# Attention steps handed out in groups of two or three between dense products, in a one-core decoder block

## The chip, the core and the metric

The kernel runs on one core of a Trainium2 chip. TensorE (PE in the rows, with PEld for its weight loads) multiplies matrices into PSUM banks; VectorE (DVE), ScalarE (ACT) and GpSimd (POOL) read those banks or SBUF and do the element-wise work; SyncE (SP) issues most transfers. Each engine has its own instruction order and waits on semaphores for the others. The metric is the device time of one execution in microseconds, lower is better: the median of 3 runs before the change is 640.49 us (640.24 to 640.78).

## The reference

One decoder block on 512 tokens of width 1024, all in float32:

```python
hn = rms_norm(x, norm_g)
proj = hn @ w_in                      # q, k, v, forget logits, gate
q = rms_norm(q, q_gain); k = rms_norm(k, k_gain)
o_moba = moba_attention(...)          # heads 0-3
o_fox  = forgetting_attention(...)    # 6 heads
o_dil  = dilated_attention(...)       # 6 heads
y_moba = rms_norm(o_moba); y_fox = rms_norm(o_fox) * sigmoid(g_fox); y_dil = rms_norm(o_dil)
x = x + concat([y_moba, y_fox, y_dil]) @ w_out
x = x + square(relu(rms_norm(x) @ w_up)) @ w_down
```

There are 16 heads of width 64. All three kinds of attention are causal and reduce here to softmax(q k / 8 + a bias per head) v over the 512 tokens, the bias being a table for ten heads and a cumulative sum of log-sigmoids for the six forgetting heads.

## The kernel before, in words

**Dense products.** Every float32 operand is split into a high part and a remainder (whi and wlo for weights, xh and xl, y0h and y0l and so on for activations), and a product is three matmuls: high by high, high by remainder, remainder by high. One k index of one output bank, three matmuls, is called a token here. The generator `product` (L247) yields after each token. Its order is: the first two k for each of four banks in turn, then the middle k, then the last two k for each bank; a bank's `done` function is called after its last token. The input projection is nine chunks of 32 tokens (`IN_CHUNKS`, L41): q and k of four heads (512 columns), v of four heads (256 or 262 columns), in turn, and last the gate g (384 columns). The output projection is four products: 20, 20, 12 and 12 tokens of 512 columns. The first two take k = 0, 1 (group 0 of heads, y0) and k = 5, 6, 7 (group 1, y1); the last two take k = 2, 3, 4 (group 2, y2). Behind it come the up and down products, with no attention between.

**Attention steps.** Each head is 12 steps, each a short run of TensorE work followed by work on other engines:

- stack (two per head, L486): four transposes of q or k, copied by ScalarE;
- s (four, L508): scores of one 128-row block into a bank, bias and minimum on VectorE (L526), exponential on ScalarE (L528), which is the last reader of the bank;
- pt (three, L536): 4, 3 and 3 transposes of the probabilities, copied by ScalarE to pth (L547), remainder by VectorE to ptl (L548);
- av (two, L553): pth and then ptl times v into one bank, copied by ScalarE (L570);
- o (one, L575): four transposes, a sum on VectorE (L582), a product on GpSimd (L589). The o step of a group's last head also calls `group_norm` (L599): squares on ScalarE (L605), a small chain on VectorE (L608, then `rsqrt`), and four row scalings on VectorE (L612 or L616).

Beside these there are y steps, four per group (`y_transpose`, L618: transposes, a ScalarE copy to the high part, L625, a VectorE remainder, L626), and steps with little or no TensorE work (root and norm of q and k, sig, and f for the cumulative sum). A step is written below with head and index, as s 13.2; y 2.3 is the fourth y step of group 2.

**Banks.** All attention steps take their bank from a ring of four ("m"); the dense products take theirs from another four ("acc"). A fifth step can write only when the readers of the first are done.

**The order.** TensorE's order is the program's own; the instructions of the other engines are ordered by the framework's scheduler. After each token the program calls `attend` (L688), a planner that runs when the kernel is built. It keeps a clock of its own (token and step costs), and a step is eligible when the steps that it needs lie a fixed lag back on that clock (`LAG`, L631). A credit grows with each token (1.2 per token of 512 columns in the input projection, in proportion for narrower ones; 2.75 in the output projection) up to 3.0. A TensorE step costs 1.0, a step without TensorE work 0.25. `attend_until` (L700) issues steps with no token between until a named one is out: the o step of the last head of group 1 (head 9) and the y steps of group 1 after the input projection (L761 to L766), and sig and the y steps of group 2 (L770, L771) after the second product of the output projection.

Of the kernel before, what the change touches and what calls it, by code (L numbers as in the profile page):

```python
# [156 lines left out]
def hymba_block(ctx: ExitStack, tc: tile.TileContext, a, out):  # L157
# [513 lines left out]
    credit = 0.0  # L671
    issued = {}

    def eligible(s):
        for key, lag in s[2]:
            if key[1] >= 0:
                if key not in issued or issued[key] + LAG[lag] > clock:
                    return False
        return True

    def issue(s):
        nonlocal clock
        steps.remove(s)
        s[1]()
        clock += COST[s[0][0]]
        issued[s[0]] = clock

    def attend(rate, cost):  # L688

        nonlocal clock, credit  # L690
        clock += cost
        credit = min(credit + rate, 3.0)
        while credit >= 1.0:
            s = next((s for s in steps if eligible(s)), None)
            if s is None:
                return
            issue(s)
            credit -= 1.0 if COST[s[0][0]] else WEIGHT
# [9 lines left out]
    for c, (kind, i) in enumerate(IN_CHUNKS):  # L708
        done = {"g": lambda i: g_done, "qk": lambda i: qk_parts[i][0], "v": v_done}[kind](i)
        n = a[f"w_in{c}"].shape[2]  # L710
        for _ in product(in_first[c], list(range(NK)), in_operands(n), NT, done):
            tokens += 1
            if tokens == STATS_AT:
                x_stats()
            attend(RATE * n / 512, TOKEN * n / 512)
        issued[kind, i] = clock
# [50 lines left out]
    for c, part, ks in OUT_ORDER[:2]:  # L767
        for _ in product(out_first[c, part], ks, out_operands, 4, out_done(c, part)):
            attend(RATE2, TOKEN)
# [250 lines left out]
```

## Time and profile before

| what | us |
| --- | --- |
| median of 3 runs | 640.49 |
| the profiled execution | 639.8 |
| its span, first to last instruction | 638.0 |
| TensorE busy in it | 627.6 |
| VectorE busy in it | 460.2 |
| ScalarE busy in it | 322.4 |

The profiled execution's own time is its span and 1.8 us around it. A timeline row gives the start of the first of a run of like instructions, the time to the end of the last, and in brackets how long the engine was idle before it and who ended that. The ends of matmuls are modelled and overlap the next one's start, so the pace of TensorE is read from start to start.

### The profile page before, as it was taken

What the parts mean: (1) busy time and instruction counts of PE and PEld (TensorE: products, weight loads), DVE (VectorE), ACT (ScalarE), POOL (GpSimd) and SP (SyncE); (2) the same over time, 40 slices, a digit from 0 to 9 for tenths busy, and PEclk for the clock granted to TensorE, in tenths of its full rate; (3) what the DMA queues carried; (4) which work ended last, traced back from release to release, by engine and by line L of the source; (5) the groups of instructions that cost most, each with busy time, mean ns of one, the idle gap of its engine ahead of it and who ended that gap; (6) DMA issues with size and microseconds to landing.
All of it is one profiled execution on the core that took longest, in us unless ns stands there. A gap on an engine that the chain in (4) does not pass through costs nothing.

```text
span 638.0 us, 9834 instructions
## 1 busy us (share of the span) xinstructions
PE 627.6 (98%) x3800; PEld 556.3 (87%) x3800; DVE 460.2 (72%) x786; ACT 322.4 (51%) x575; POOL 43.9 (7%) x63
## 2 busy tenths in 40 slices
PE   7999999999999999999999999999999999999997
PEld 5798898898889998888888989898988989988986
DVE  6794695696688565678899676686578765966872
ACT  7457666676777575549543433343434343433320
POOL 4010210130120100002100000000000000000000
PEclk9999999999999999999999999999999999999999
DMA  8524423323422345167425233422530333212213
GB/s 313 161 96 133 123 84 76 125 75 116 134 63 71 106 136 155 51 230 175 107 72 164 84 111 100 131 68 67 166 100 22 144 100 133 66 37 64 67 43 123
DMA packets 24911, 70.03 MB, mean 110 GB/s; under 512 B 3210, under 2 KB 4762, under 8 KB 24864
## 3 DMA queue, kind: packets, MB, share of 16 engines
q1 hardware_dynamic: 18224, 57.84, 28.5%
q10 hardware_dynamic: 4432, 5.77, 3.7%
q0 software_dynamic: 2208, 5.79, 3.7%
q8 instruction: 30, 0.49, 0.3%
q14 instruction: 17, 0.14, 0.1%
HBM read 61.51 MB, written 2.11 MB: 100 GB/s over the span
## 4 chain that ended last, share of the span: by engine, by line
PE 77%; DVE 7%; ACT 1%; issue 1%; ACTq 0%; POOL 0%; DVEq 0%
PE acc L913 28%; PE m L872 22%; PE acc L274 20%; PE m L514 2%; PE m L565 2%; PE m L541 1%; DVE ptl L548 1%; PE m L495 1%; DVE qkss L400 1%; DVE wlo L119 1%; DVE qks L418 1%; DVE m L526 1%; DVE qkraw L413 1%; DVE qkv L401 1%; DVE osum L582 0%
## 5 line engine op out<-in xcount | busy, mean ns | idle before, releaser
L118 ACT CAST whi<-wraw 128x1024 fp32r<-128x1024 f32 (+3 forms) x66 | 66.7, 1014 | 90.5 <-PE acc L913 39.9
L274 PE MATMUL acc<-whi,xh 128*128 128x512 f32 (+3 forms) x284 | 103.4, 364 | 0.7 <-DVE fl L436 0.4
L913 PE MATMUL acc<-hh,wlo 128*128 128x512 f32 x256 | 101.5, 396 | 0.0
L913 PE MATMUL acc<-hh,whi 128*128 128x512 f32 x256 | 101.3, 396 | 0.0
L913 PE MATMUL acc<-hl,whi 128*128 128x512 f32 x256 | 101.2, 395 | 0.0
L119 DVE TENSOR_TENSOR wlo<-wraw,whi 128x1024 fp32r<-128x1024 f32 (+3 forms) x66 | 78.8, 1195 | 29.6 <-ACT whi L118 28.9
L274 PE MATMUL acc<-wlo,xh 128*128 128x512 f32 (+3 forms) x284 | 95.7, 337 | 2.2 <-DVE wlo L119 2.2
L274 PE MATMUL acc<-whi,xl 128*128 128x512 f32 (+3 forms) x284 | 95.8, 337 | 0.0
L872 PE MATMUL m<-zh,whi 128*128 128x256 f32 x224 | 62.5, 279 | 0.0
L872 PE MATMUL m<-zl,whi 128*128 128x256 f32 x224 | 62.3, 278 | 0.0
L872 PE MATMUL m<-zh,wlo 128*128 128x256 f32 x224 | 62.3, 278 | 0.0
L274 PEld LDWEIGHTS acc<-wlo,xh 128*128 128x128 f32 x284 | 54.0, 190 | 5.3 <-DVE wlo L119 3.0
L274 PEld LDWEIGHTS acc<-whi,xl 128*128 128x128 f32 x284 | 53.6, 189 | 5.1
L913 PEld LDWEIGHTS acc<-hh,wlo 128*128 128x128 f32 x256 | 48.3, 189 | 11.0 <-DVE wlo L119 0.3
L913 PEld LDWEIGHTS acc<-hl,whi 128*128 128x128 f32 x256 | 48.3, 189 | 10.3 <-issue 0.2
L913 PEld LDWEIGHTS acc<-hh,whi 128*128 128x128 f32 x256 | 48.3, 189 | 10.1 <-ACT m L882 0.2
L274 PEld LDWEIGHTS acc<-whi,xh 128*128 128x128 f32 x284 | 53.7, 189 | 3.7 <-DVE vs L430 0.7
L922 DVE TENSOR_TENSOR x<-acc,x 128x512 f32<-128x512 f32 (+1 forms) x65 | 42.6, 676 | 10.3 <-PE acc L913 9.6
L118 ACT CAST whi<-wsum 128x1024 fp32r<-128x1024 f32 x28 | 29.4, 1049 | 40.1 <-PE m L872 40.1
L119 DVE TENSOR_TENSOR wlo<-wsum,whi 128x1024 fp32r<-128x1024 f32 x28 | 34.2, 1221 | 19.6 <-ACT whi L118 19.6
L528 ACT ACTIVATE p<-m,mn 128x128 f32<-128x128 f32 (+1 forms) x64 | 33.6, 527 | 24.6 <-DVE mn L526 22.9
L872 PEld LDWEIGHTS m<-zh,whi 128*128 128x128 f32 x224 | 42.1, 188 | 1.2
(193 smaller groups left out, 1323.5 us busy)
## 6 DMA issues: line engine op xcount, KB each, us to landing
wraw<-in_w_down SPq DMA_DIRECT2D x32, 512.0 KB, 3.6
ublk<-in_w_up SPq DMA_DIRECT2D x28, 512.0 KB, 3.8
wraw<-in_w_in SPq DMA_DIRECT2D x21, 512.0 KB, 3.8
stk<-stk ACTq DMA_DIRECT2D x32, 128.0 KB, 2.4
wraw<-in_w_out SPq DMA_DIRECT2D x6, 512.0 KB, 4.1
alibi<-in_alibi POOLq DMA_DIRECT2D x10, 256.0 KB, 3.0
x<-in_xT SPq DMA_DIRECT2D x4, 512.0 KB, 5.5
wraw<-in_w_up SPq DMA_DIRECT2D x4, 512.0 KB, 5.1
```

Source lines behind the costliest of these rows:

```text
L118: nc.scalar.copy(hi, raw)
L119: nc.vector.tensor_tensor(lo, raw, hi.bitcast(F32), op=ALU.subtract)
L274: nc.tensor.matmul(dst, lhsT=lhs, rhs=rhs, start=(k == 0 and m == 0), stop=(k == n - 1 and m == 2))
L400: nc.vector.tensor_reduce(ss, sq.rearrange("p (h d) -> p h d", d=DH), axis=AX.X, op=ALU.add)
L401: nc.vector.tensor_scalar(state["v"][:, t], ss, 1.0 / DH, eax[:, t : t + 1], op0=ALU.mult, op1=ALU.add)
L413: nc.vector.tensor_tensor(raw, raw, state["y"][:, t].unsqueeze(2).broadcast_to([P, 8, DH]), op=ALU.mult)
L514: nc.tensor.matmul(ps[:, :n], lhsT=st[0][:, i * P : (i + 1) * P], rhs=st[m][:, :n], start=(m == 1), stop=(m == 2 and h < FOX0),)
L528: nc.scalar.activation(p, ps[:, :n], AF.Exp, bias=mn, scale=-1.0, accum_out=st["den"][:, i : i + 1])
L565: nc.tensor.matmul(ot[:, j * P :], lhsT=v, rhs=p, start=(half == 0 and j == 0), stop=(half == 1 and j == 3))
L872: nc.tensor.matmul(acc[:, f * HALF : (f + 1) * HALF], lhsT=lhs, rhs=rhs, start=first and (f, j, m) == (0, 0, 0), stop=(f, j, m) == (1, 3, ...
L913: nc.tensor.matmul(acc, lhsT=lhs, rhs=rhs, start=(p, k, m) == (0, 0, 0), stop=(p, k, m) == (1, 1, 2))
L922: nc.vector.tensor_tensor(dst[:, cols], acc[:, cols], dst[:, cols], op=ALU.add)
```

## The change

`attend` now returns when the credit is below 2.0. A step is handed out only when at least two have come due, and then the loop runs as before, until less than one is left. Rates, costs, lags and the cap are unchanged.

```diff
     def attend(rate, cost):
 
+
         nonlocal clock, credit
         clock += cost
         credit = min(credit + rate, 3.0)
+        if credit < 2.0:
+            return
         while credit >= 1.0:
             s = next((s for s in steps if eligible(s)), None)
```

Three lines are added, so everything below stands three lines further down in the changed kernel (L745 becomes L748).

In TensorE's order, the first attention work is the stacking of heads 0 to 2, in the second q and k chunk (L495 are the transposes of stack steps, four to a step; L274 are tokens of the dense product, three rows to one). Before:

```order
L495 MATMUL m<-identr,qks 128x128 x12
L274 MATMUL acc<-whi,xh 128x512
L274 MATMUL acc<-wlo,xh 128x512
L274 MATMUL acc<-whi,xl 128x512
L495 MATMUL m<-identr,qks 128x128 x4
L274 MATMUL acc<-whi,xh 128x512
L274 MATMUL acc<-wlo,xh 128x512
L274 MATMUL acc<-whi,xl 128x512
L495 MATMUL m<-identr,qks 128x128 x4
```

Now:

```order
L495 MATMUL m<-identr,qks 128x128 x12
L274 MATMUL acc<-whi,xh 128x512
L274 MATMUL acc<-wlo,xh 128x512
L274 MATMUL acc<-whi,xl 128x512
L274 MATMUL acc<-whi,xh 128x512
L274 MATMUL acc<-wlo,xh 128x512
L274 MATMUL acc<-whi,xl 128x512
L495 MATMUL m<-identr,qks 128x128 x8
```

Single steps one token apart have become pairs two tokens apart. Over the whole program the same 205 TensorE steps stand in 94 groups instead of 150, so 111 steps follow another step directly instead of 55.

At TensorE's end of the attention work, in the second product of the output projection (L622 are the transposes of the y steps of group 2, three to a step, y1h and y1l operands of the second product, y2h and y2l of the third), before:

```order
L622 MATMUL m<-ident,o_187 128x128 x9
L274 MATMUL acc<-y1h,whi 128x512
L274 MATMUL acc<-y1l,whi 128x512
L274 MATMUL acc<-y1h,wlo 128x512
L622 MATMUL m<-ident,o_187 128x128 x3
```

Behind these stood three more tokens on y1 and then the first on y2. Now:

```order
L274 MATMUL acc<-y1h,whi 128x512
L274 MATMUL acc<-y1l,whi 128x512
L274 MATMUL acc<-y1h,wlo 128x512
L622 MATMUL m<-ident,o_187 128x128 x12
L274 MATMUL acc<-y2h,whi 128x512
L274 MATMUL acc<-y2l,whi 128x512
L274 MATMUL acc<-y2h,wlo 128x512
```

The four y steps have moved behind the last token on y1 and directly ahead of the first on y2. The o step of head 15, which they need, has moved from 18 tokens ahead of the first y2 token (14, 1 and 3) to 13.

On VectorE at the same place (orr and rs_t belong to the group norm's small chain, L612 scales the rows of o, the x rows add a finished output bank, L626 makes the remainders y2l), now:

```order
L748 TENSOR_TENSOR x_2914<-acc,x_2914 128x512
L289 TENSOR_TENSOR rs_t<-rs_t,orr 128x4
L290 SCALAR_TENSOR_TENSOR orr<-rs_t,orr 128x4
L288 SCALAR_TENSOR_TENSOR rs_t<-orr,ov 128x4
L289 TENSOR_TENSOR rs_t<-rs_t,orr 128x4
L290 SCALAR_TENSOR_TENSOR orr<-rs_t,orr 128x4
L748 TENSOR_TENSOR x_2914<-acc,x_2914 128x512
L612 SCALAR_TENSOR_TENSOR o_187<-o_187,orr,gsig 128x384 x4
L748 TENSOR_TENSOR x_2914<-acc,x_2914 128x512 x2
L626 TENSOR_TENSOR y2l<-m,y2h 128x3x128 x4
```

Before, two weight remainders (L123) stood inside the small chain where two additions to x stand now; the two additions between L612 and L626 stood there before too.

At the other end of the second half, where the input projection ends, the planner has 35 attention steps left to place among the 40 tokens of the first two output products, against 22 before: head 12 from its pt steps on, s 13.3, stack 15.0, s 14.0 to s 14.2 and the first two pt steps of head 13 have slipped past that point. TensorE's order there, now (L622 are the y steps of group 1, L541 the transposes of pt 12.0 to 12.2):

```order
L274 MATMUL acc<-whi,xl 128x384
L622 MATMUL m<-ident,o_186 128x128 x12
L274 MATMUL acc<-y0h,whi 128x512
L274 MATMUL acc<-y0l,whi 128x512
L274 MATMUL acc<-y0h,wlo 128x512
L541 MATMUL m<-ident,p_2842 128x128
L541 MATMUL m<-ident,p_2849 128x128
L541 MATMUL m<-ident,p_2856 128x128
L541 MATMUL m<-ident,p_2873 128x128
```

Before, the o step of head 12 stood directly ahead of these y steps, and the pt step behind the first token was the last one of head 13.

## Rows read from the trace of the kernel before

**Rows 1.** The page: busy time, share of the span and instructions per engine.

```profile
PE 627.6 (98%) x3800; PEld 556.3 (87%) x3800; DVE 460.2 (72%) x786; ACT 322.4 (51%) x575; POOL 43.9 (7%) x63
```

**Rows 2.** Stretches: busy us (instructions) per engine, clock, DMA share, GB/s.

```profile
27.00:236.00 209.00, 207.31 (x1367) 188.08 (x1367) 150.30 (x388) 141.12 (x324) 28.98 (x43) 1.00 0.35 102
236.00:263.30 27.30, 27.25 (x158) 23.16 (x156) 16.96 (x37) 16.96 (x35) 1.83 (x3) 1.00 0.38 117
315.00:638.00 323.00, 319.54 (x1952) 284.77 (x1950) 234.88 (x279) 117.76 (x143) 0.00 (x0) 1.00 0.29 92
```

**Rows 3.** TensorE timeline, two stalls: start, us, instruction, idle before.

```profile
83.80 0.44 PE L514 MATMUL m<-stk,stk 128*128 128x128 f32 x2 [0.39 <-DVE ptl L548]
...
206.82 0.34 PE L274 MATMUL acc<-whi,xl 128*128 128x384 f32 x1
207.75 0.85 PE L565 MATMUL m<-pth,vs 128*128 128x512 f32 x4 [0.59 <-DVE ptl L548]
```

**Rows 4.** TensorE timeline, three stack steps together and one alone.

```profile
48.37 1.15 PE L495 MATMUL m<-identr,qks 128*128 128x128 f32 x12
...
49.65 0.39 PE L274 MATMUL acc<-wlo,xh 128*128 128x512 f32 x1
...
50.11 0.46 PE L495 MATMUL m<-identr,qks 128*128 128x128 f32 x4
...
50.71 0.39 PE L274 MATMUL acc<-wlo,xh 128*128 128x512 f32 x1
```

**Rows 5.** Groups of weight loads on TensorE: busy us, mean ns of one, idle.

```profile
L495 PEld LDWEIGHTS m<-identr,qks 128*128 128x128 f32 x128 | 13.8, 140 | 2.4
```

**Rows 6.** TensorE timeline around the last attention steps.

```profile
262.98 0.60 PE L580 MATMUL m<-ident,ots 128*128 128x128 f32 x4
...
273.04 1.14 PE L622 MATMUL m<-ident,o 128*128 128x128 f32 x9
...
277.12 0.39 PE L274 MATMUL acc<-y2h,whi 128*128 128x512 f32 x1
```

**Rows 7.** The chain that ended last, same stretch: start, us, what.

```profile
263.14 0.44 PE m L580 x4
263.57 9.63 PE acc L274 x42
...
274.88 0.33 PE m L622 x3
```

**Rows 8.** VectorE timeline, same stretch.

```profile
264.23 0.69 DVE L582 TENSOR_REDUCE osum<-m 128x256 f32<-128x512 f32 x1
...
267.81 0.17 DVE L608 TENSOR_SCALAR ov<-oss 128x4 f32<-128x4 f32 x1 [2.90 <-ACT ots L605]
...
271.19 2.21 DVE L612 SCALAR_TENSOR_TENSOR o<-o,orr,gsig 128x384 f32<-128x384 f32 x4
273.32 1.28 DVE L745 TENSOR_TENSOR x<-acc,x 128x512 f32<-128x512 f32 x2
274.52 1.94 DVE L626 TENSOR_TENSOR y2l<-m,y2h 128x384 fp32r<-128x384 f32 x4
```

**Rows 9.** ScalarE timeline, same stretch.

```profile
273.57 1.25 ACT L625 CAST y2h<-m 128x384 fp32r<-128x384 f32 x3 [4.56 <-PE m L622]
275.25 0.48 ACT L625 CAST y2h<-m 128x384 fp32r<-128x384 f32 x1 [0.43 <-PE m L622]
```

**Rows 10.** TensorE timeline where the input projection ends.

```profile
236.06 1.95 PE L622 MATMUL m<-ident,o 128*128 128x128 f32 x12
237.76 0.48 PE L274 MATMUL acc<-y0h,whi 128*128 128x512 f32 x1
...
238.79 0.71 PE L514 MATMUL m<-stk,stk 128*128 128x512 f32 x2
239.34 0.22 PE L519 MATMUL m<-diag,identr 128*128 128x128 f32 x1
239.40 0.44 PE L274 MATMUL acc<-y0h,whi 128*128 128x512 f32 x1
```

**Rows 11.** ScalarE timeline, the exponential of that s step (s 14.3).

```profile
241.13 0.69 ACT L528 ACTIVATE p<-m,mn 128x512 f32<-128x512 f32 x1
```

## The prediction

> **What bounds the kernel now.** I read the busy table first: TensorE is busy for 627.6 of 638.0 us, the next engine, VectorE, for 460.2 [rows 1]. Modelled matmul ends flatter a busy TensorE, so I went on to the stretches. From 27 to 236 us, where attention steps lie between the tokens of the input projection, TensorE is idle for 209.00 - 207.31 = 1.69 us in all; from 236 to 263.3 us it is idle for 0.05 us, and from 315 us on there is no attention left [rows 2]. The granted clock is 1.00 in each. So the attention half is bound by TensorE's own instructions, and VectorE and ScalarE (150 and 141 of 209 us) have room on average. What is left to win there is small. The idle column names four stalls; I take two as samples. One token before s 3.0 can write, the bank that it wants is still read by a pt remainder (idle 0.39), and av 11.0 waits 0.59 for another [rows 3]. A stall costs somewhat more than its idle time: the second has 207.75 - 206.82 = 0.93 from start to start, where a matmul of 384 columns takes 0.18 (0.525 for a token of three), so 0.75 is lost for 0.59 idle [rows 3]. For four stalls that makes 1.69 + 4 x 0.16 = 2.3 us. A fifth loss is not in the idle column: the four y steps of group 1 take 237.76 - 236.06 = 1.70 us where 12 transposes at the 0.11 of other y steps (0.33 for three [rows 7]) take 1.32, so 0.4 us of bank waits [rows 10]. Sum: 2.7 us of waits in the whole attention half.
>
> Third, I looked at what each handover between dense and attention work costs. Three stack steps together: from their start to the second dense matmul 49.65 - 48.37 = 1.28 us, less 0.23 for the dense matmul between, 1.05, or 0.35 a step; one alone: 50.71 - 50.11 - 0.23 = 0.37 [rows 4].
>
> **The change part by part.** No instruction is added or removed; only positions move. SP's and POOL's transfers keep their order but for a bias table some steps earlier or later, and the tables are asked for heads ahead, so I cost them at nothing (cover: the lag of 5.5 planner units between stack and s; if it were gone, one DMA per head would show as an s stall).
>
> (a) *Fewer handovers.* 56 more steps follow another step directly. A joined stack step saves 0.37 - 0.35 = 0.02 us [rows 4]. The other kinds have no shuffle of this size in the rows shown, so I bound them between 0 and 0.02 and take half: 56 x 0.01 = -0.6 us, bounds 0 and -1.1.
>
> The Trainium skill speaks against this term ("TensorE: Matmul & The Clock Gate", section "Step-by-step: what each phase is for"): weight loads are pulled ahead, so that the next weights load while the present matmul runs. A load takes 140 ns [rows 5], and in the run of twelve a transpose takes 1.05 / 12 = 88 ns, so by that rule a step behind another would show some 50 ns that a dense matmul of 512 columns hides: 56 x 0.05 = +2.8 us. The rows have it the other way, -20 ns, so the sum goes by the rows and the rule becomes a rival.
>
> (b) *The end of attention.* This is the largest term. Before: the o step of head 15 starts at 262.98. Its consumers run in a chain: head sum 264.23, squares on ScalarE, the small chain from 267.81, row scalings 271.19 to 273.40, two additions to x to 274.60, the four remainders y2l to 274.52 + 1.94 = 276.46 [rows 8]. So the last y2l is ready 13.5 us after the o step starts. Over this lie 14 + 1 + 3 tokens and four y steps, and the first matmul on y2 starts at 277.12, that is 14.1 us after it [rows 6], and uses y2h; the second uses y2l. There are 0.66 + 0.23 = 0.9 us to spare. Now only 13 tokens lie between, at 9.63 / 42 x 3 = 0.69 us each [rows 7], the o step is 0.44 [rows 7], and four y steps are 4 x 0.33 [rows 7]: TensorE arrives at the first y2 matmul 0.44 + 8.97 + 1.32 = 10.7 us after the o step's start, and at the second at 10.9. The y steps themselves barely wait (the first row scaling is done 271.19 + 0.55 - 262.98 = 8.8 us after the o step, the last 10.4; TensorE reaches them from 9.4 to 10.4). But the chain is as long as before: VectorE has two additions where it had two weight remainders, and the two additions ahead of y2l are still there, the last of them waiting for the last token itself. So y2l is ready at about 13.5, and 13.5 - 10.9 = 2.6 us of TensorE time are lost; nothing dense stands between. Lower bound: if y2l overtook the queue and only y2h counted. Its last copy ended at 275.25 + 0.48 = 275.73 [rows 9], 0.85 us after the last y step's start at 274.88 [rows 7], and where four copies of 0.42 (1.25 / 3) queue behind one another it is some 1.4, so at least 1.2 us with one remainder behind it. Upper bound: 1 us more, if the chain starts behind ScalarE's weight copies: 3.6. I take +2.7.
>
> (c) *The start of the output projection.* 35 steps instead of 22 must go among its tokens, at two or three per single token (rate 2.75), so a step comes back to a bank of the ring of four sooner. A score step frees its bank at the end of its exponential: s 14.3 left TensorE at 239.40 and its exponential ended at 241.13 + 0.69 = 241.82, 2.4 us later [rows 10, 11]. In the new order y 1.3 wants the bank of s 13.2 after one 384-column token and three y steps, 0.52 + 1.0 = 1.5 us; s 14.2 wants that of s 13.3 after stack 15.0, a token and two short s steps, 0.37 + 0.69 + 0.7 = 1.75; pt 13.2 that of s 14.3 after 1.8, s 15.3 that of pt 14.1 after 1.9. Four waits of 0 to 0.9 us; the one of s 14.2 is the worst, since its exponential also stands behind three pt copies. At 2.0 us for a narrower s (0.5), 2.4 (0.65 for s 14.2, 0.6 for pt 13.2) and little for the last (0.1) they make 1.8; the y waits of before, 0.4, are replaced by the first. Net +1.4, bounds 0 (all absorbed, as in the stretch 236 to 263.3 now) and +2.5.
>
> (d) *Inside the input projection.* Of the 2.3 us of stalls, the one before s 3.0 goes (eight tokens now stand between pt 2.2 and it), the others are tied to chunk ends and to VectorE's load and may stay. What is late next: the pattern of three pt steps, two tokens, an s step, an s step, where the second s wants the first pt's bank 2.4 to 2.5 us later; before, 2.55 us was too short once, for s 3.0 [rows 3]. I take -0.3, bounds -2.3 and +3.3 (six such places at 0.55).
>
> Sum: -0.6 + 2.7 + 1.4 - 0.3 = +3.2 us. On the profiled execution's 639.8 (span 638.0 and 1.8 around it) that is 643.0; the median of the runs is 0.7 higher, so I forecast 643.7.
>
> **The rivals.**
>
> *Everything is absorbed and stalls vanish (not slower).* If groups give VectorE and ScalarE longer quiet stretches, all 2.3 us of stalls and the 0.4 at the y steps go, joins save 0.6, (c) is zero, and (b) is at its lower bound: 640.5 - 3.3 + 1.2 = 638.4. For it: VectorE is busy for only 72% of the stretch. Against it: the end of attention is a chain of latencies, not a load. It decides at a y2l ready within 1.2 us of the last y step.
>
> *The tail is at its lower bound and the rest cancels:* 640.5 - 0.6 + 1.2 - 0.3 + 0.2 = 641.0, or less if one more stall goes: within 0.2% of before.
>
> *Groups of three starve the bank ring inside the input projection:* (d) at +3.3 instead of -0.3 makes 647.3. For it is the stall of s 3.0; against it that runs of three pt steps stand in the order of before already and only one of them stalled a successor.
>
> *Exposed weight loads:* +2.8 instead of -0.6 in (a), 140 ns less 88 for every further join [rows 4, 5], makes 647.1; rows 4 speak against it. It is the rule of the skill named above.
>
> That the change does nothing is excluded by the order: 150 groups have become 94.
>
> **How the numbers follow.** Forecast with (b) as worked out and (c) between its bounds: 0.73, own range 642.0 to 645.5. Ring starved: 0.08. Exposed loads: 0.03. Cancelling: 0.10, of which I count two thirds within 0.2% (1.3 us, about what a measurement here can tell from no change) and a third above. All absorbed: 0.06, faster. So slower 0.73 + 0.08 + 0.03 + 0.03 = 0.87, same 0.07, faster 0.06. The range 641.2 to 646.2 leaves out the two long cases, the fast one and a part of the cancelling one, under 0.2 together.
>
> **What would show it.** (b): an idle time of TensorE of 1 to 3 us before the first or second matmul on y2, ended by VectorE's y2l, and none there before. (c): the stretch from the y steps of group 1 to the o step of head 15 longer than its steps and tokens, with idle times ended by L528, L547 or L548. (a): three stack steps still at 1.05 us, two at 0.72. (d): four or fewer stalls of 0.3 to 0.8 us before the y steps of group 1. The prediction is wrong if y2l is ready before TensorE arrives, or if the sum of idle times inside the input projection moves by more than 1.5 us.

## Result and profile after

The changed kernel takes 643.97 us (median of 4 runs, 642.99 to 645.33) against 640.52 for the kernel before: ratio 1.0057, 95% interval 1.0045 to 1.0069. In a second series it took 643.66 (5 runs) against 640.62, ratio 1.0051 (1.0039 to 1.0064). It is slower by 0.5 to 0.6%, about what was forecast (643.7). But of the four terms only two had about the right size; the other two missed in opposite directions. Some executions of the changed kernel took 1.2 to 2.3 us more than others of the same series, no profile fell in one of them, and why they do is open.

The profiled execution took 642.99 us (span 641.2), 3.2 more than that of before. The page's busy times and the stretches that answer to [rows 1, 2] (27 us to the y steps of group 1, and from there to the o step of head 15):

```profile
PE 628.2 (98%) x3800; PEld 556.6 (87%) x3800; DVE 457.8 (71%) x786; ACT 322.9 (50%) x575; POOL 44.1 (7%) x63
```

```profile
27.00:231.30 204.30, 201.98 (x1323) 183.41 (x1323) 143.51 (x374) 134.59 (x305) 28.54 (x42) 1.00 0.35 99
231.30:268.00 36.70, 36.45 (x219) 31.35 (x217) 22.30 (x52) 23.64 (x53) 2.38 (x4) 1.00 0.42 135
```

All engines have the same work as before. In the input projection TensorE is idle for 204.30 - 201.98 = 2.32 us (1.69 before), in the output projection's first stretch for 0.25 (0.05 before), both at granted clock 1.00. What is left lies at the end of attention. TensorE's timeline there (start, us, instruction, idle before and who ended it), which answers to [rows 6]:

```profile
267.60 0.60 PE L580 MATMUL m<-ident,ots 128*128 128x128 f32 x4
...
276.95 1.47 PE L622 MATMUL m<-ident,o 128*128 128x128 f32 x12
279.20 0.51 PE L274 MATMUL acc<-y2h,whi 128*128 128x512 f32 x1 [0.78 <-ACT y2h L625]
280.57 0.50 PE L274 MATMUL acc<-y2l,whi 128*128 128x512 f32 x1 [0.87 <-DVE y2l L626]
```

TensorE comes to the y steps 9.35 us after the o step of head 15 began and then waits twice, for y2h and for y2l. From start to start these two cost 1.03 and 1.15 us more than where nothing waits, 2.17 together. VectorE at the same place, which answers to [rows 8]:

```profile
268.23 0.69 DVE L582 TENSOR_REDUCE osum<-m 128x256 f32<-128x512 f32 x1 [3.63 <-PE m L580]
...
272.11 0.17 DVE L608 TENSOR_SCALAR ov<-oss 128x4 f32<-128x4 f32 x1 [1.23 <-ACT ots L605]
...
275.26 2.20 DVE L612 SCALAR_TENSOR_TENSOR o<-o,orr,gsig 128x384 f32<-128x384 f32 x4
277.38 1.28 DVE L748 TENSOR_TENSOR x<-acc,x 128x512 f32<-128x512 f32 x2
278.57 1.95 DVE L626 TENSOR_TENSOR y2l<-m,y2h 128x384 fp32r<-128x384 f32 x4
```

The chain is that of before, two additions to x ahead of y2l included. It ends at 280.52, 12.9 us after the o step's start (13.5 before), and TensorE's matmul on y2l starts 0.05 us later. ScalarE, which answers to [rows 9], copies y2h behind two weight conversions:

```profile
276.24 1.41 ACT L122 ACTIVATE whi<-wraw,gains 128x512 fp32r<-128x512 f32 x2 [4.16 <-PE acc L274]
277.55 1.60 ACT L625 CAST y2h<-m 128x384 fp32r<-128x384 f32 x4
```

The handovers, TensorE's timeline at two joined stack steps (answers to [rows 4]):

```profile
50.91 0.79 PE L495 MATMUL m<-identr,qks 128*128 128x128 f32 x8
51.54 0.47 PE L274 MATMUL acc<-whi,xh 128*128 128x512 f32 x1
51.85 0.39 PE L274 MATMUL acc<-wlo,xh 128*128 128x512 f32 x1
```

51.85 - 50.91 - 0.23 = 0.71 us for two, where two single ones took 0.74.

Inside the input projection the waits of before at 83.80 and 207.75 [rows 3] are gone, and others have come. Four of them:

```profile
109.78 1.44 PE L514 MATMUL m<-stk,stk 128*128 128x128 f32 x6
...
113.84 0.44 PE L514 MATMUL m<-stk,stk 128*128 128x128 f32 x2 [0.75 <-ACT p L528]
...
200.14 0.85 PE L565 MATMUL m<-pth,vs 128*128 128x512 f32 x4 [0.34 <-DVE ptl L548]
...
225.40 0.30 PE L514 MATMUL m<-stk,stk 128*128 128x128 f32 x1 [1.04 <-DMA stk<-stk]
```

The first shows no idle time, but its six matmuls (s 4.0 to s 4.2) take 1.44 us, where the same six take 0.97 in another order (below): 0.47 lost. s 5.0 loses 0.92 at 113.84, av 10.0 loses 0.50 at 200.14, and s 12.0 loses 1.20 at 225.40. ScalarE and then VectorE ahead of the first two:

```profile
107.89 0.42 ACT L605 ACTIVATE ots<-o 128x256 f32<-128x256 f32 x1 [1.76 <-POOL o L589]
...
109.50 1.05 ACT L497 CAST stk<-m 128x512 fp32r<-128x512 f32 x2
...
113.33 0.37 ACT L528 ACTIVATE p<-m,mn 128x128 f32<-128x128 f32 x1 [1.42 <-DVE mn L526]
```

```profile
109.63 0.17 DVE L608 TENSOR_SCALAR ov<-oss 128x4 f32<-128x4 f32 x1 [2.25 <-ACT ots L605]
...
111.89 1.14 DVE L616 TENSOR_SCALAR o<-o,orr 128x256 f32<-128x256 f32 x4
112.94 0.29 DVE L526 CUSTOM_DVE_ANT_0 m<-m,alibi 128x128 f32<-128x128 f32 x1
```

The norm of group 0 (squares L605, small chain L608, scalings L616) stands ahead of the stack copies on ScalarE and of the bias of s 4.0 on VectorE. That bias starts 112.94 - 109.78 = 3.2 us after the scores that it reads, and the exponentials that free the ring follow from 113.33.

From the 97th matmul of L274 to its last (start to start; the last stands in the first 32 tokens of the up product) TensorE takes 280.61 us before and 283.93 now, 3.3 more. Of that -0.7 are handovers (all attention steps without their waits: 84.6 us before, 83.9 now), +2.17 the end of attention, about +0.1 the first stretch of the output projection, less than 0.1 a wait for a weight remainder at 297.44 (0.17, of which 0.11 was there before), and the rest, +1.7, new waits in the input projection less those that went.

### The profile page after: what moved, and what is told of

Read it like the earlier page. It is cut to its first block, busy times and chain, and to the rows that moved or that the text cites. A ratio compares the mean times of both kernels' runs of the same rounds, so it can differ in the third digit from the quotient of the medians.

```text
span 641.2 us, 9808 instructions
## 1 busy us (share of the span) xinstructions
PE 628.2 (98%) x3800; PEld 556.6 (87%) x3800; DVE 457.8 (71%) x786; ACT 322.9 (50%) x575; POOL 44.1 (7%) x63
## 4 chain that ended last, share of the span: by engine, by line
PE 56%; DVE 0%; DVEq 0%; issue 0%
PE acc L916 28%; PE m L875 22%; PE acc L274 6%; PE m L828 0%; DVE x L925 0%; DVEq L1019 0%
## 5 line engine op out<-in xcount | busy, mean ns | idle before, releaser
L274 PE MATMUL acc<-whi,xh 128*128 128x512 f32 (+3 forms) x284 | 100.1, 352 | 0.0
L274 PE MATMUL acc<-wlo,xh 128*128 128x512 f32 (+3 forms) x284 | 95.7, 337 | 2.1 <-DVE wlo L119 2.1
L274 PE MATMUL acc<-whi,xl 128*128 128x512 f32 (+3 forms) x284 | 95.6, 337 | 0.0
L274 PEld LDWEIGHTS acc<-wlo,xh 128*128 128x128 f32 x284 | 53.8, 189 | 6.5 <-DVE wlo L119 3.2
L274 PEld LDWEIGHTS acc<-whi,xl 128*128 128x128 f32 x284 | 53.6, 189 | 5.2
L274 PEld LDWEIGHTS acc<-whi,xh 128*128 128x128 f32 x284 | 53.7, 189 | 3.7 <-DVE vs L430 0.2
L875 PEld LDWEIGHTS m<-zl,whi 128*128 128x128 f32 x224 | 42.0, 187 | 1.2
```

The lines of the kernel that those rows point to most:

```text
L274: nc.tensor.matmul(dst, lhsT=lhs, rhs=rhs, start=(k == 0 and m == 0), stop=(k == n - 1 and m == 2))
L875: nc.tensor.matmul(acc[:, f * HALF : (f + 1) * HALF], lhsT=lhs, rhs=rhs, start=first and (f, j, m) == (0, 0, 0), stop=(f, j, m) == (1, 3, ...
```

## Experiments

Two theories. *Fixed waits:* holding steps back makes attention run late, so that 13 tokens instead of 18 cover the last chain (2.2 us), and steps meet the norm of group 0 and the weight loads at a worse moment (1.7 us). *Grouping as such:* groups of two and three fill the ring of four banks faster than it is emptied. The threshold can only act in the input projection: in the output projection one token's credit is 2.75, always above 2.0. The letters in each run's expectation are that run's own, and each ratio is against the kernel before in the same series.

**Grouped, with a credit of 1.3 per token.**

```diff
-    RATE, RATE2 = 1.2, 2.75
+    RATE, RATE2 = 1.3, 2.75
```

> Groups of two or three as in the changed kernel, but with a rate of 1.3 steps per 512-column token instead of 1.2, so that the planner has 21 steps left at the end of the input projection (35 in the changed kernel, 22 before) and 18 tokens lie between the o step of head 15 and the first matmul on y2 (13 and 18). Theory A (the backlog uncovers the last chain): no idle time of TensorE before y2, about 2.2 us less than the changed kernel; with its other waits kept, 641.3 to 641.9. Theory B (grouping itself costs the time, by waits on banks, copies and transfers inside the input projection): 643 or more. Theory C (A holds, but the higher rate brings waits of its own): between the two.

646.38 us (644.05 to 647.08), ratio 1.0082. The cover is back and the wait for y2 gone, as theory A of that run said, but the total is not in its range: it lies where theory B had it, since new waits came. TensorE's waits (engine, line, for what: us idle, times, longest):

```profile
PE m L495 <- DVE qks L418: 1.9, 1, 1.9
...
PE m L622 <- DVE ptl L548: 0.9, 1, 0.9
```

The stack step of head 12 arrives before the norm of its q and k is done, and y 1.2 before the bank that it wants is free. Whether the rate or the grouping is to blame is not told by this run; the last one takes the two apart.

**The kernel before, arriving late at the end.**

```diff
-            attend(RATE * n / 512, TOKEN * n / 512)
+            attend((0.6 if kind == "g" else RATE) * n / 512, TOKEN * n / 512)
```

> Steps one by one as in the kernel before, but with a rate of 0.6 instead of 1.2 in the last chunk of the input projection alone, so that 35 steps are left at its end as in the changed kernel and 12 tokens lie between the o step of head 15 and the first matmul on y2. Theory A (the backlog uncovers the last chain): two waits of TensorE, for y2h and y2l, of 2.2 to 3.2 us together, and 642.7 to 643.7, with no grouping. Theory B (grouping costs the time): 640.5, within 0.3.

648.42 us (647.63 to 649.94), ratio 1.0121. Without any grouping TensorE loses 2.46 us to y2h and y2l, as A had it; B falls. The rest of the loss was not foreseen. On ScalarE the sigmoid of the gate with its two table loads came between two exponentials, 4.05 us in all, and s 15.1 waited 2.4 us for a bank:

```profile
246.45 1.28 ACT L468 ACT_TABLE_LOAD   x1
247.75 1.49 ACT L468 ACTIVATE gsig<-gsig 128x1536 f32<-128x1536 f32 x1
249.25 1.28 ACT L528 ACT_TABLE_LOAD   x1
```

And the granted clock fell behind both waits (see the last section). So this run shows that lateness alone makes the tail wait, but its total isn't clean.

**Groups of three.**

```diff
-        if credit < 2.0:
+        if credit < 3.0:
```

> The threshold is 3.0 instead of 2.0: always three steps. 45 steps are left at the end of the input projection, and no token is left between the o step of head 15 and the y steps. Theory A: nothing covers the last chain any more, so TensorE waits for 13.5 - 0.44 - 1.32 - 0.23 = about 11.5 us less what a quiet VectorE saves, 9 to 11.5, and the kernel takes 650 to 653. Theory B (waits grow with the size of the groups, not with the backlog): 2 to 4 us above the changed kernel, 646 to 648.

653.62 us (651.87 to 654.08), ratio 1.0194, 0.6 above A's interval and far above B's. From the o step of head 15 to the third matmul on y2 TensorE takes 12.0 us for some 2.2 of work, 9.8 lost, as A had it, though part of it is a lower clock and not waiting. Head 15 ends so late that no dense token is left to cover its norm. TensorE's timeline:

```profile
285.30 2.79 PE L622 MATMUL m<-ident,o 128*128 128x128 f32 x12 [7.10 <-DVE o L612]
```

**Only the y steps of group 2 earlier.**

```diff
-            step(("y", g, t), partial(y_transpose, g, t), [(("o", GROUPS[g][1] - 1, 0), "norm")])
+            step(("y", g, t), partial(y_transpose, g, t), [(("o", GROUPS[g][1] - 1, 0), "norm2")])
```

The new lag "norm2" is 7 planner units instead of 9.

> The changed kernel with a lag of 7 instead of 9 for the y steps of group 2 alone: they go out after 11 and 12 of the 13 tokens instead of directly ahead of the first matmul on y2; the o step of head 15 stays where it is. Theory A (the chain from the o step to y2l is what counts, 13.5 us long, under 13 tokens): the wait moves ahead of the y steps or stays before y2, the total stays, 643.2 to 644.2. Theory D (the y steps standing directly ahead of their use are what costs): the waits of 2.2 us shrink by half or more, 642.0 to 642.8.

643.33 us (642.56 to 645.58), ratio 1.0041. The total is where A had it, but the wait only halved, to 1.26 us: part of it moved to the y steps, which now come before their rows are scaled, and half a microsecond stays at y2l. The chain is 0.6 shorter, 12.3 us from the o step (269.19) to the last y2l (281.49), because only one addition to x stands ahead of y2l. What was won at the end does not show in the profiled execution (644.23): its order is that of the changed kernel up to there, yet s 8.0 lost 1.3 us to a swap, where it lost 0.3.

```profile
277.59 1.58 PE L622 MATMUL m<-ident,o 128*128 128x128 f32 x9 [0.26 <-DVE o L612]
...
281.55 0.50 PE L274 MATMUL acc<-y2l,whi 128*128 128x512 f32 x1 [0.24 <-DVE y2l L626]
```

**The end alone.** On the kernel before, the pt steps of head 15 get a longer lag.

```diff
-            needs = [(("s", h, i), "s") for i in {i for _, i in BANKS[b]}] + [(("av", h - 1, 1), "free")]
+            needs = [(("s", h, i), "late" if h == 15 else "s") for i in {i for _, i in BANKS[b]}] + [(("av", h - 1, 1), "free")]
```

> The order of before up to the last pt step of head 14: steps are still handed out one by one. Only the three pt steps of head 15 are held by a longer lag (6.5 instead of 3.5 planner units), so that the o step of head 15 lies 13 tokens ahead of the first token on y2, as after the change, instead of 18. This does the second part of the prediction (the end of attention) alone. Theory A (the chain of 13.5 us from that o step to y2l costs what its cover lacks, whatever the grouping): TensorE waits for y2h and y2l together about 2.2 us, as after the change (2.17), the rest of the trace as before, total 642.5 to 643.5 us (before, 640.7, and 2.2; up to 1.5 more in executions where the granted clock falls behind the wait). Theory B (the end costs only together with grouping, since the groups ahead of it leave ScalarE and VectorE behind): waits below 0.7 us and 640.5 to 641.2.

642.39 us (642.05 to 644.22), ratio 1.0034 (1.0022 to 1.0046): 1.8 us by the medians, 2.2 by the ratio. TensorE's timeline repeats that of the changed kernel to 0.05 us, with single steps all the way to head 14:

```profile
266.48 0.60 PE L580 MATMUL m<-ident,ots 128*128 128x128 f32 x4
...
278.08 0.49 PE L274 MATMUL acc<-y2h,whi 128*128 128x512 f32 x1 [0.78 <-ACT y2h L625]
279.48 0.50 PE L274 MATMUL acc<-y2l,whi 128*128 128x512 f32 x1 [0.91 <-DVE y2l L626]
```

From the 97th to the last matmul of L274 it takes 282.89 us, 2.28 above before. This settles the largest term: 13 tokens of cover cost 2.2 us by themselves. The total is 0.1 below A's interval; B falls.

**The changed kernel with o steps handed out at once.**

```diff
         if credit < 2.0:
-            return
+            s = next((s for s in steps if eligible(s)), None)
+            if s is None or s[0][0] != "o":
+                return
```

> After the change, but an o step that has come due is handed out even when the credit is below 2.0; all others still wait for two. The o step of head 15 then lies 17 tokens ahead of the first token on y2 instead of 13, with 25 attention steps left at the end of the input projection instead of 35. Theory A (of the 3.5 us that the change costs, 2.2 are this missing cover and 1.5 are waits inside the input projection): y2 waits 0 to 0.3 us, other waits of some 3 to 4 us stay, total 641.0 to 642.3. Theory B (grouping as such costs the time, by whatever waits its groups bring): other waits rise by what the tail gives back, total 643 or more.

643.54 us (642.27 to 645.65), ratio 1.0053. The first y2 matmuls start without a wait, as A said, but the total missed A's interval and lies where B put it. From the 97th to the last matmul of L274 it takes 283.36 us, 0.6 below the changed kernel, so 1.6 of the 2.2 us came back as other waits, most of them in the input projection:

```profile
169.16 0.93 PE L514 MATMUL m<-stk,stk 128*128 128x128 f32 x5 [2.06 <-DMA stk<-stk]
...
208.77 0.45 PE L274 MATMUL acc<-whi,xh 128*128 128x384 f32 x1 [0.87 <-DVE vs L430]
...
213.02 0.62 PE L495 MATMUL m<-identr,qks 128*128 128x128 f32 x5 [0.55 <-DVE qks L418]
```

None of these three is a wait for a bank of the ring (0.57 us at s 15.0, in the output projection, is). They are for the swapped halves of a stack, for the dense product's own bank, and for a norm: work whose time does not follow the planner's clock.

**The changed kernel, norm of group 0 sooner.**

```diff
-        step(("o", h, 0), o_step(h), [(("av", h, 1), "av"), (("o", h - 1, 0), "free")])
+        step(("o", h, 0), o_step(h), [(("av", h, 1), "av3" if h == 3 else "av"), (("o", h - 1, 0), "free")])
```

The new lag "av3" is 1.5 instead of 3.

> After the change, but the o step of head 3 (with the norm of group 0) has a lag of 1.5 instead of 3 planner units, so that it stands two tokens earlier in TensorE's order; the end of the order is that of after the change. Theory A (the waits of 1.4 us at the s steps of heads 4 and 5, 109.8 to 113.8 us after the change, come from the norm's squares on ScalarE and its small chain on VectorE, which stand ahead of the copies and exponentials that these s steps wait for): these waits fall to 0.0 to 0.5, the y2 waits stay at 2.2, total 642.5 to 643.1. Theory B (the waits come from groups of steps that fill the ring of four banks faster than it is emptied): they stay at 1.0 to 1.6 and the total at 643.5 to 644.0.

643.60 us (642.99 to 643.73), ratio 1.0044. The waits at s 4.0 to s 5.0 vanished altogether, so they did come from the norm. But the total stayed where B had it, 0.06 below the changed kernel of the same series. TensorE, then VectorE:

```profile
117.48 0.66 PE L541 MATMUL m<-ident,p 128*128 128x128 f32 x4 [0.77 <-DVE y0l L626]
```

```profile
115.86 1.23 DVE L119 TENSOR_TENSOR wlo<-wraw,whi 128x1024 fp32r<-128x1024 f32 x1 [1.11 <-ACT whi L118]
117.00 1.41 DVE L626 TENSOR_TENSOR y0l<-m,y0h 128x256 fp32r<-128x256 f32 x4
```

Four microseconds on, a pt step waits for a bank that y0l still reads, because the conversion of a weight chunk stood ahead of it. Of 1.4 us some 0.5 was won in this stretch, too little for this measurement to tell.

**The changed kernel again,** in the same series.

> The changed kernel once more, as the yardstick of this series. Theory A (cost of the change is fixed waits: 2.2 us at the end, 1.5 inside the input projection): the same places wait again, the y2h and y2l waits within 0.3 us of 2.17, those at 109.8 to 113.8 within 0.4 of 1.4, the two waits for stack transfers (0.28 and 1.20 us in the first profile) may move by 1 us either way; total 643.0 to 645.0, where the upper part belongs to executions in which the granted clock falls for some us behind a wait. Theory B (the cost is mostly that of the transfers, by chance): the sum of waits inside the input projection moves by more than 1.5 us and the total with it.

643.66 us (642.99 to 645.22). The same places wait: 2.15 us at y2, 1.4 at s 4.0 to s 5.0, 1.45 at s 12.0 (1.20 in the first profile). A holds.

**Grouping in one chunk only, the third of q and k.**

```diff
-        if credit < 2.0:
+        if credit < least:
...
-            attend(RATE * n / 512, TOKEN * n / 512)
+            attend(RATE * n / 512, TOKEN * n / 512, 2.0 if c == 4 else 0.0)
```

> Steps wait for a second one only in the third q and k chunk (heads 4 to 6 are stacked there, tokens 130 to 161); everywhere else they are handed out one by one as before. The s steps of heads 4 and 5 then stand in the same groups of three and two as after the change, but the o step of head 3 stands seven tokens ahead of them as before, not five, and the end of attention is that of before (22 steps left, 18 tokens of cover). 11 joins more than before. Theory A (the 1.4 us of waits at these s steps after the change came from the norm of group 0 arriving late, because earlier chunks had held steps back; groups by themselves cost nothing): no wait over 0.5 us at s 4.0 to s 5.0, other waits as before, total 640.3 to 640.9. Theory B (groups of three and two s steps fill the ring of four banks and wait, whatever stands ahead): 0.9 us or more at s 5.0, total 641.4 to 642.2.

640.65 us (11 runs) against 640.15, ratio 1.0007 (0.9998 to 1.0015). The same groups of s steps as in the changed kernel run without a wait for the ring:

```profile
109.32 0.97 PE L514 MATMUL m<-stk,stk 128*128 128x128 f32 x6
...
111.50 0.79 PE L514 MATMUL m<-stk,stk 128*128 128x512 f32 x4
...
141.81 0.30 PE L514 MATMUL m<-stk,stk 128*128 128x128 f32 x1 [0.64 <-DMA stk<-stk]
```

B falls here. The o step of head 3 started 6.6 us ahead of these s steps instead of 5.0. Some 32 us on, a new wait for a swap costs more than the joins gave (0.8 us; not in A's list).

**Grouping in the gate chunk only.** The same edit with `kind == "g"`.

> Steps wait for a second one only in the last chunk of the input projection (the gate, 384 columns, credit 0.9 per token); everywhere else as before. 11 joins more; 23 steps left instead of 22 and 17 tokens of cover at the end instead of 18. The stack steps of heads 12 to 14 come in pairs here too, five tokens ahead of s 12.0, beside the same weight load. Theory A (the wait for the swapped halves of stack 12 after the change, 1.2 us, comes from chance: that a weight load was issued right ahead of the swap there): no wait over 0.4 us at s 12.0, the wait of 0.75 at av 11.0 stays, total 640.2 to 641.0. Theory B (pairs of stack steps bring the swaps so close that they land late by themselves): 0.8 us or more at s 12.0, total 641.3 to 642.2.

640.65 us, ratio 1.0008 (0.9999 to 1.0018). There is no wait at s 12.0, though its stack steps come in pairs: B falls as stated. Transfers by issue, for the weight load and the two swaps of head 12 (KB each, median us from issue to landing), of this kernel:

```profile
wraw<-in_w_out SPq DMA_DIRECT2D x1, 512.0 KB, 4.0
...
stk<-stk ACTq DMA_DIRECT2D x2, 128.0 KB, 3.4
```

and of the changed kernel:

```profile
wraw<-in_w_out SPq DMA_DIRECT2D x1, 512.0 KB, 6.0
stk<-stk ACTq DMA_DIRECT2D x2, 128.0 KB, 4.2
```

In the changed kernel the load was issued between the two swaps, which landed after 2.3 and 6.0 us, and two more swaps were issued 1.4 and 1.9 us behind the second. Here the load went 0.9 us ahead of the first, and the next two swaps followed 1.7 and 2.3 us behind the second. A also listed the wait at av 11.0, which stayed; not listed was 1.0 us at y 1.3, whose bank y1l still read.

**Single steps with a credit of 1.3,** the control for the first run.

```diff
-    RATE, RATE2 = 1.2, 2.75
+    RATE, RATE2 = 1.3, 2.75
```

> The kernel before with a credit of 1.3 per token instead of 1.2, steps handed out one by one: 19 steps left at the end of the input projection and 22 tokens of cover at the end. It is the control for the run that had 1.3 with grouping (646.4 us). Theory A (grouping brings the waits; the higher rate by itself only moves steps a little earlier): waits of 2 to 3.5 us in the input projection, none at the end, total 640.0 to 641.8. Theory B (the higher rate by itself makes steps come ahead of what they need): waits of 5 us or more, total 643.5 or more.

639.75 us (639.06 to 640.47) against 640.15, ratio 0.9991 (0.9982 to 0.9999), just below A's interval. Its waits (two for swaps, 0.9 and 1.2 us lost; av steps 0.6 and 0.4) add up to 3.1 us, as A had it:

```profile
PE m L514 <- DMA stk<-stk: 1.8, 2, 1.0
...
PE m L565 <- DVE y1l L626: 0.4, 1, 0.4
```

So the rate by itself was not what cost 646.4, and with 22 tokens of cover the end is free. Against the kernel before of its series, grouping at this rate took 5.5 us more and single steps 0.4 less: here grouping costs 5.9 us with nothing lost at the end. This is the only kernel of the study below the kernel before, by 0.4 us, with an interval that just excludes no change.

## Why the forecast held, step by step

- *(a), -0.6:* -0.7 measured. That is 0.01 us a join, 0.03 for the pair of stack steps above. The Trainium skill ("TensorE: Matmul & The Clock Gate", section "Step-by-step: what each phase is for") says that the next weights load while the present matmul runs; the prediction estimated from it that a step behind another would show a part of its loads, +2.8. The trace has the opposite sign, so the rival of exposed loads falls.
- *(b), +2.7:* 2.17, and 2.2 when done alone. The mechanism was right in each part: cover of 13 tokens, the two additions still ahead of y2l, y2l as the last thing awaited. It was 0.5 too large because the chain took 12.9 us, not 13.5 (squares and small chain each some 0.2 to 0.3 sooner). The sign that it named, an idle time ended by y2l, came second: the first wait is for y2h, whose four copies run from 277.55 to 279.15. The prediction had this queue of copies in its lower bound only; as y2l comes later still, it adds nothing to the sum.
- *(c), +1.4:* about +0.1, at its lower bound. Of the four bank waits of 0 to 0.9 us only that at y 1.3 came (0.42), in place of the 0.4 of before. For pt 13.2 I took the wait of one exponential, 2.4 us after its scores [rows 10, 11]; this time it took 1.9 (241.79 to 243.65). For s 14.2, the worst of the four, the bank was not the one that I named. TensorE at y 1.3 and s 14.2, then ScalarE's exponential of s 13.3:

```profile
232.76 0.55 PE L622 MATMUL m<-ident,o 128*128 128x128 f32 x3 [0.25 <-ACT p L528]
...
238.14 0.56 PE L514 MATMUL m<-stk,stk 128*128 128x384 f32 x2
```

```profile
237.94 0.69 ACT L528 ACTIVATE p<-m,mn 128x512 f32<-128x512 f32 x1 [0.42 <-DVE mn L526]
```

The exponential of s 13.3 ends 2.4 us after its scores, as forecast, at 238.63. But s 14.2 writes from 238.14 on, so it writes another bank. Unlike what the description of the ring and the prediction say, the four banks are not always taken in turn, and a wait found by counting four steps back need not come.
- *(d), -0.3:* +1.7, inside the bounds of -2.3 to +3.3 but with the wrong sign. The idle time, by which the prediction wanted to see it, rose by only 0.6: matmuls that wait for late stack copies show no idle mark, and each stall costs more than its idle time. The stalls that I left standing, at chunk ends and at 207.75, went; new ones came. I looked for waits on the ring among pt and s steps. They came from what holding back does to the rest: the norm of group 0 ahead of head 4's copies, and swaps that land late: that of stack 12 beside a weight load (6.0 us) and, with 0.3 lost, that of stack 8 behind two bias broadcasts of 256 KB from GpSimd (5.6 us).
- *The sum* was right by luck: (c) and (d) missed by -1.3 and +2.0 and (b) by -0.5, and these cancel.
- *Rivals:* "all absorbed" and "cancelling" fall by the tail alone. "Ring starved" fails as a mechanism (grouping in one chunk), though the sign that it gave (d) was right.

What stays open: what exactly made that one swap take 6.0 us was not separated (load, or four swaps close together). Late swaps are not new: in the kernel before, the four transfers of the swaps at 165 and 241 us landed after 4.4 to 5.3 us, and nothing waited for them. Nor is it known how much grouping must lose in the input projection: it lost 1.7 us in the changed kernel, more in the kernel with a credit of 1.3, and little with one chunk grouped. That these waits come from the norm is shown for those at s 4.0 to s 5.0 alone; for the others the cause is read from the trace.

## What to carry to other kernels

When steps are held back to be batched, first count what covers the last chain of the phase, from its producer to its first use: here that loss could be worked out beforehand to half a microsecond, and a batching gain of 0.01 us a step did not pay for it. Waits in the middle of this tightly packed schedule could not be forecast from one pattern: removing one (2.2 us at the end, 1.4 at the s steps) brought up others (1.6 and 0.9), so judge a reordering by its end-to-end time, not by the wait that it removes. A control with the other half of an edit (the rate without the grouping) was worth more than any of the repairs.

## What the runs showed of the hardware

The granted clock of TensorE fell from 2.4 to 1.2 GHz around long waits, in the stretches below, and dense matmuls of 512 columns in them took nearly twice as long (0.43 against 0.23 us from start to start in the late single-step kernel). Stretches of the late single-step kernel (columns as in [rows 2]), behind a wait of 2.4 us that ended at 251.27 and behind those at y2, then of the groups of three, in the second half of a wait of 7.1 us:

```profile
252.00:255.50 3.50, 3.50 (x14) 3.10 (x14) 1.12 (x5) 2.02 (x8) 0.00 (x0) 0.51 0.00 0
...
286.00:290.00 4.00, 4.00 (x11) 3.13 (x12) 1.76 (x3) 0.00 (x0) 0.00 (x0) 0.57 0.86 289
```

```profile
281.50:288.30 6.80, 2.79 (x12) 2.39 (x12) 5.41 (x18) 2.35 (x8) 0.00 (x0) 0.50 0.24 77
```

Behind the two waits of 0.8 and 0.9 us of the changed kernel's profile it stayed at 1.00.

A transfer of 128 KB for a swap landed after 2.2 to 2.4 us on quiet queues. In the two profiles of the changed kernel it took 4.3 to 6.3 us beside or behind the weight load ahead of s 12.0, and 5.5 to 5.9 behind two bias broadcasts ahead of s 8.0; the longest of the study took 7.7 (groups of three). And one Sigmoid among exponentials cost ScalarE two table loads of 1.28 us beside its own 1.49.
